# First norm's shift and scale weights of layer 0 in four units of two feature tiles, with four open sums in the first projection

## The chip, the cores and the metric

The kernel runs on one core of one Trainium2 chip. The metric is the device time of one execution in microseconds (us). The core's engines are TensorE (PE, matmuls; PEld its weight loads), VectorE (DVE), ScalarE (ACT) and GpSimd (POOL); SyncE (SP) issues nearly all DMAs, in program order on one queue.

## What is computed

A two-layer backbone over 256 latent and 256 context tokens with 1024 features. Layer 0 is a windowed attention and a bidirectional gated recurrence (HGRN2) side by side, layer 1 a retention; each layer ends with a SwiGLU feed-forward. Every sub-layer starts with an RMS norm whose result is modulated with a shift and a scale that come from a conditioning vector:

```python
for layer in range(DEPTH):
    m_lat = split((silu(c) @ mod_w[layer] + mod_b[layer]), 6)      # shift, scale, gate; shift, scale, gate
    m_ctx = split((silu(c_ctx) @ mod_w[layer] + mod_b[layer]), 6)
    h_lat = rms_norm(x, norm_g[layer, 0]) * (1.0 + m_lat[1]) + m_lat[0]
    h_ctx = rms_norm(ctx, norm_g[layer, 0]) * (1.0 + m_ctx[1]) + m_ctx[0]
    y_ctx, y_lat = mixer(h_ctx, h_lat, ...)                        # even or odd layer, h @ w_in first
    x = x + m_lat[2] * y_lat
    x = x + m_lat[5] * swiglu(rms_norm(x, norm_g[layer, 1]) * (1 + m_lat[4]) + m_lat[3], ...)
    # the same for ctx in layer 0
return x
```

## The kernel before

Activations lie with features on the 128 partitions: 8 feature tiles of 512 columns, 256 latent (`LAT`) and 256 context (`CTX`). All arithmetic is fp32. A dense product is made of three matmuls: each weight piece (8 blocks of 128x128, 512 KB, tile `raw`) is split into `whi` (ScalarE, L268) and `wlo` (VectorE, L269), each activation into `hh` or `u` (high) and `hl` or `u` (low), and L336, L337 and L338 multiply high by high, low by high and high by low. `ensure` makes the pieces `LOOK` = 2 ahead of the piece that is used; `raw` has three buffers, `whi` and `wlo` four. The order of the 230 pieces is the order in which `take` asks for them.

The start is written out by hand (`manual_schedule`), in the order in which each engine is to run it. SP loads constants (`con`), x (8 DMAs), the context (4 DMAs) and then `mw0`, the 8 MB of weights for layer 0's first shift and scale, as 32 tiles of 256 KB in four units: scale of feature tiles 0 to 3, scale of 4 to 7, shift of 0 to 3, shift of 4 to 7. ScalarE squares x and context, VectorE adds the squares, one matmul per stream with a matrix of ones sums them (L453), and Ln and Exp make 1/rms. `mod0a(nt)` multiplies the conditioning (`cT`, 32 columns) by a unit (L175, 8 matmuls), a copy takes the sum out of PSUM (L178), `mod0b(nt)` turns it into columns (L185, 4 matmuls of 2 columns) and adds the bias (L154, L158). `scaled` (L459) multiplies a feature tile by 1/rms and scale, `shifted` (L465, L466) adds the shift and splits it into `hh` and `hl`. Only then come the dense projections of the even layer:

```python
p1 = group('ein', [E_AK, E_AQ], K8, HS, sls=(LAT, CTX))
start('q', qk_post([(p1[0], 1, kt), (p1[1], 0, qt)]))
p2 = group('ein', [E_AQ + 1, E_AQ + 2, E_AQ + 3, E_AV], K8, HS, kouter=False)
```

The first has two columns of blocks in 128x256 halves, the second four columns of 128x512. The work that hangs on them runs in lanes (`qk_post`, `v_post`, the attention, the HGRN heads), generators that step once per tick; `work` makes a tick for every `TICK` = 1600 columns that the dense matmuls stream. The weights of the other shifts, scales and gates (`mwT`, 80 tasks of 512 KB) are reduced on VectorE at ticks too: `mod_tick` starts one task (two passes of L233 for the two streams) every `modt` ticks (`MODE` = 2.3 in the even layer; `MODT` later), and `mod_until` runs what is left of it at the end of a mixer. The token-major group (`tokgroup`, L409 to L411) follows the second projection. L567 and L578 are the small matmuls of `qk_post`, L483 is the residual update, L524 the silu of the conditioning `cb`.

Of the kernel before, what the change touches and what calls it, by code (L numbers as in the profile page):

```python
# [7 lines left out]
F32 = mybir.dt.float32  # L8
# [8 lines left out]
P = 128  # L17
# [18 lines left out]
MODT = [4.6, 5.5, 4, 4]  # L36
# [4 lines left out]
MODE = 2.3  # L41
# [27 lines left out]
def hybrid_kernel(ctx, tc, xT, wst, mw0, mwT, small, cbc, cst, imask, dmat, out, order):  # L69
# [47 lines left out]
    for i in range(32):
        if 16 <= i < 22:
            if i % 2 == 0:
                pair = rawp.tile([P, 2, NT], F32, tag="raw", name=nm("raw"))  # L120
            t = pair[:, i % 2, :]
        elif 22 <= i < 28:
            if i % 2 == 0:
                pair = mp.tile([P, D], F32, tag="mr", name=nm("mr"))
            t = pair[:, (i % 2) * NT:(i % 2 + 1) * NT]
        elif i < 16:
            t = u()[:]
        else:
# [42 lines left out]
    def mod0a(nt):  # L171
        ps = axb()
        for k in range(KD):
            g = k % 4
            T.matmul(ps[32 * g:32 * g + 32, :], cT[:, k, :], mws[nt * 8 + k], start=(k < 4), stop=(k >= 4),  # L175
                     skip_group_check=True)
        parts[nt] = u()
        A.activation(parts[nt][:], ps[:], AF.Copy)  # L178

    def mod0b(nt):  # L180
        ch, half = 1 - nt // 2, nt % 2
        part = parts[nt]
# [3 lines left out]
        mod_finish(0, ch, half * 4, half * 4 + 4, ps2[:].rearrange("p c s -> p s c"))  # L186
# [73 lines left out]

    def ensure(p):
        for q in range(len(pieces), min(p + LOOK, N_PIECE - 1) + 1):
            r = q
            load_raw(r)
            src = raws.pop(r)
# [153 lines left out]
    class Norm:  # L419
# [6 lines left out]
        def pre(self, k):  # L426
# [5 lines left out]
            A.activation(hi[:, LAT], x[k][:], AF.Copy, scale=g)  # L432
            V.scalar_tensor_tensor(lo[:, LAT], x[k][:], g, hi[:, LAT].bitcast(F32), ALU.mult, ALU.subtract)
# [98 lines left out]

# [786 lines left out]
```

## Time and profile before

| | us |
|---|---|
| median of three runs (lowest, highest) | 1146.19 (1146.14, 1147.27) |
| the profiled execution | 1146.45 |
| its span, first to last instruction | 1144.6 |
| PE busy in the span | 1116.4 (98%) |
| DVE busy | 767.4 (67%) |
| ACT busy | 554.0 (48%) |

Times in the rows are microseconds from the span's start. A matmul counts as busy for its modelled length, so a busy PE may still be waiting for a tick of another engine's work; the distance between starts is what a matmul costs. A fp32 matmul that is not split shows as two records.

### The profile page before, as it was taken

To read this page: it belongs to the slowest core of one execution; us is meant where nothing else is said; L and a number is where in the kernel's file an instruction comes from. 1 tells how busy PE (TensorE), PEld (TensorE's weight loads), DVE (VectorE), ACT (ScalarE), POOL (GpSimd) and SP (SyncE) were. 2 spreads that over 40 slices of the span, in tenths; PEclk is the share of its full clock that TensorE was granted. 3 is DMA by queue.
4 is the path that set the end of the run, shared out by engine and by line. 5 is a ranking of instruction groups with operands and counts; after the bars stand their busy time and mean duration, and the time that the engine had idled before them with its cause. 6 is when DMAs were issued, how large, how long until landed. Compare 5 with 4: busy or idle time off the path is not lost.

```text
span 1144.6 us, 18866 instructions
## 1 busy us (share of the span) xinstructions
PE 1116.4 (98%) x7514; PEld 996.9 (87%) x7514; DVE 767.4 (67%) x1399; ACT 554.0 (48%) x948; POOL 20.8 (2%) x46
## 2 busy tenths in 40 slices
PE   3999999999999999999999998999999999999998
PEld 1777877888998888988888898999999999999998
DVE  3877698899798557357883678374646577555553
ACT  5676676664753231123322476454445657544441
POOL 0012000000000000000000000000000000000000
PEclk9999999999999999999999999999999999999999
DMA  9987221326237446247983324343434265655553
GB/s 329 349 235 184 92 65 66 112 74 202 94 113 241 143 147 202 77 139 237 324 308 109 95 75 129 111 131 109 148 94 147 92 203 167 192 183 181 184 183 109
DMA packets 56121, 182.46 MB, mean 159 GB/s; under 512 B 6368, under 2 KB 9824, under 8 KB 55904
## 3 DMA queue, kind: packets, MB, share of 16 engines
q1 hardware_dynamic: 53648, 176.45, 47.6%
q0 software_dynamic: 2240, 4.72, 1.7%
q8 instruction: 59, 0.97, 0.4%
q14 instruction: 30, 0.25, 0.1%
q10 hardware_dynamic: 144, 0.08, 0.0%
HBM read 177.56 MB, written 1.05 MB: 156 GB/s over the span
## 4 chain that ended last, share of the span: by engine, by line
PE 84%; DVE 10%; ACT 3%; DMA 1%; issue 1%; DVEq 0%; ACTq 0%; SPq 0%
PE mm L338 23%; PE mm L337 23%; PE mm L336 23%; PE ax L337 2%; PE ax L336 2%; PE ax L338 2%; DVE wlo L269 2%; DMA raw<-in_wst_dram 1%; PE ax L175 1%; PE ax L656 1%; ACT whi L268 1%; PE ax L675 1%; DVE u L459 1%; PE mm L411 1%; PE mm L409 1%
## 5 line engine op out<-in xcount | busy, mean ns | idle before, releaser
L268 ACT ACTIVATE whi<-raw 128x1024 fp32r<-128x1024 f32 x230 | 243.3, 1059 | 403.0 <-PE mm L337 242.9
L269 DVE TENSOR_TENSOR wlo<-raw,whi 128x1024 fp32r<-128x1024 f32 x230 | 280.7, 1222 | 166.5 <-ACT whi L268 165.9
L336 PE MATMUL mm<-hh,whi 128*128 128x256 f32 (+1 forms) x1072 | 362.2, 339 | 1.2 <-ACT whi L268 0.9
L338 PE MATMUL mm<-hh,wlo 128*128 128x256 f32 (+1 forms) x1072 | 361.6, 338 | 0.6 <-DVE wlo L269 0.6
L337 PE MATMUL mm<-hl,whi 128*128 128x256 f32 (+1 forms) x1072 | 362.0, 338 | 0.1
L337 PE MATMUL mm<-u,whi 128*128 128x256 f32 (+2 forms) x768 | 236.9, 309 | 0.0
L338 PE MATMUL mm<-u,wlo 128*128 128x256 f32 (+2 forms) x768 | 236.7, 308 | 0.0
L336 PE MATMUL mm<-u,whi 128*128 128x256 f32 (+2 forms) x768 | 236.3, 308 | 0.3 <-DVE x L483 0.3
L338 PEld LDWEIGHTS mm<-hh,wlo 128*128 128x128 f32 x1072 | 204.4, 191 | 21.8 <-DVE wlo L269 0.8
L336 PEld LDWEIGHTS mm<-hh,whi 128*128 128x128 f32 x1072 | 204.2, 191 | 21.9 <-ACT whi L268 0.9
L337 PEld LDWEIGHTS mm<-hl,whi 128*128 128x128 f32 x1072 | 204.3, 191 | 20.2 <-DVE hl L466 0.3
L336 PEld LDWEIGHTS mm<-u,whi 128*128 128x128 f32 x768 | 146.4, 191 | 7.9 <-issue 0.4
L338 PEld LDWEIGHTS mm<-u,wlo 128*128 128x128 f32 x768 | 146.6, 191 | 7.2
L337 PEld LDWEIGHTS mm<-u,whi 128*128 128x128 f32 x768 | 146.6, 191 | 7.1
L233 DVE CUSTOM_DVE_ANT_0 mr<-mr,cb 128x1024 f32<-128x1024 f32 x72 | 87.1, 1222 | 13.2 <-DMA mr<-in_mwT_dram 12.6
L416 ACT ACTIVATE u<-u 128x512 fp32r<-128x512 f32 (+1 forms) x84 | 43.0, 526 | 36.7 <-DVE u L1007 17.3
L1007 DVE TENSOR_TENSOR u<-u,mm 128x512 f32<-128x512 f32 (+1 forms) x40 | 22.1, 553 | 44.7 <-PE mm L338 44.7
L233 DVE CUSTOM_DVE_ANT_0 u<-mr,cb 128x1024 bf16<-128x1024 f32 x40 | 48.4, 1219 | 2.8 <-DMA mr<-in_mwT_dram 1.5
L417 DVE TENSOR_TENSOR u<-u,u 128x512 fp32r<-128x512 f32 (+1 forms) x84 | 46.5, 565 | 5.0 <-ACT u L416 4.9
L336 PE MATMUL ax<-u,u 128*128 128x256 f32 x160 | 45.9, 287 | 3.1 <-ACT u L416 3.1
L483 DVE SCALAR_TENSOR_TENSOR x<-mm,modv,x 128x256 f32<-128x256 f32 x48 | 22.4, 480 | 36.1 <-PE mm L338 36.1
L337 PE MATMUL ax<-u,u 128*128 128x256 f32 x160 | 46.0, 287 | 0.0
(220 smaller groups left out, 1216.4 us busy)
## 6 DMA issues: line engine op xcount, KB each, us to landing
raw<-in_wst_dram SPq DMA_DIRECT2D x230, 512.0 KB, 3.8
mr<-in_mwT_dram SPq DMA_DIRECT2D x80, 512.0 KB, 4.5
u<-in_mw_dram SPq DMA_DIRECT2D x16, 256.0 KB, 5.2
u<-u POOLq DMA_DIRECT2D x20, 128.0 KB, 5.7
u<-in_dmat_dram POOLq DMA_DIRECT2D x8, 256.0 KB, 3.0
raw<-in_mw_dram SPq DMA_DIRECT2D x6, 256.0 KB, 5.2
mr<-in_mw_dram SPq DMA_DIRECT2D x6, 256.0 KB, 5.2
x<-in_xT_dram SPq DMA_DIRECT2D x8, 128.0 KB, 3.4
```

The costliest lines, as they stand in the source:

```text
L175: T.matmul(ps[32 * g:32 * g + 32, :], cT[:, k, :], mws[nt * 8 + k], start=(k < 4), stop=(k >= 4), skip_group_check=True)
L233: V.tensor_tensor_reduce(o, mr[:], cb[:, s, :], 1.0, 0.0, ALU.mult, ALU.add, mvec(l, s, ch, k))
L268: A.activation(hi[:], src[:], AF.Copy)
L269: V.tensor_tensor(lo[:], src[:], hi[:].bitcast(F32), ALU.subtract)
L336: T.matmul(o, w[0], a[0], start=first, stop=False, skip_group_check=shared)
L337: T.matmul(o, w[0], a[1], start=False, stop=False, skip_group_check=shared)
L338: anchor[0] = T.matmul(o, w[1], a[0], start=False, stop=last, skip_group_check=shared)
L409: T.matmul(ps[t][:], a[0], w[0], start=(k == 0), stop=False)
L416: A.activation(hi, src, AF.Copy)
L417: V.tensor_tensor(lo, src, hi.bitcast(F32), ALU.subtract)
L483: V.scalar_tensor_tensor(xs(m, s), ps[:, sl], mvec(l, s, ch, m), xs(m, s), ALU.mult, ALU.add)
L1007: V.tensor_tensor(g[:, 0:w], g[:, 0:w], ps[2 * i + 1][:, 0:w], ALU.mult)
```

## The change

`mw0` is stacked so that each of the four units holds the scale and the shift of two feature tiles. The loads stand in another order: unit 0, x in two DMAs, the context in four, then a weight piece and a unit in turn. The sums of squares go to PE (16 matmuls with the matrix of ones for two), ScalarE makes six of eight squares at 512 columns and VectorE two. Each unit is multiplied, and its two feature tiles are scaled and shifted, while the projection before it runs; this projection has four columns of 512 with four open sums over all k. It calls no `work`, so no tick passes in it. The second projection keeps two columns, `qk_post` is started three times for two, `lb_consts` moves ahead, and `MODE` and `MODT[0]` are 1.9 and 4.2 for 2.3 and 4.6.

```diff
-MODT = [4.6, 5.5, 4, 4]
+MODT = [4.2, 5.5, 4, 4]
-MODE = 2.3
+MODE = 1.9
...
+    def mw_load(p):
+        mws[p] = []
+        for i in range(KD):
+            if p < 3 or i >= 6:
+                t = u()[:]
+            else:
+                if i % 2 == 0:
+                    pair = mp.tile([P, D], F32, tag="mr", name=nm("mr"))
+                t = pair[:, i % 2 * NT:i % 2 * NT + NT]
+            nc.sync.dma_start(t, mw0[p, i])
+            mws[p].append(t)
+
+    mw_load(0)
+    for j in range(2):
+        nc.sync.dma_start(xl[j][:], xT[:, 0, 4 * j:4 * j + 4, :])
     for k in range(KD // 2):
-        nc.sync.dma_start(xc[k][:], xT[:, 2 * k:2 * k + 2, CTX])
+        nc.sync.dma_start(xc[k][:], xT[:, 1, 2 * k:2 * k + 2, :])
...
-        parts[nt] = u()
-        A.activation(parts[nt][:], ps[:], AF.Copy)
+        parts[p] = ps
+    def mod0b(p):
+        part = u()
+        A.activation(part[:], parts[p][:], AF.Copy)
...
+        for i, ch in enumerate((1, 0)):
+            mod_finish(0, ch, 2 * p, 2 * p + 2, ps2[:, 2 * i:2 * i + 2, :].rearrange("p c s -> p s c"))
...
+        load_raw(0)
+        for p in range(1, 3):
+            mw_load(p)
+            load_raw(p)
+        lb_consts()
+        mod0a(0)
+        mod0b(0)
+        stat = []
         for n in ns:
-            for k in range(KD):
-                n.add(k)
-            n.stats()
+            ps = axb()[:, 0:L]
+            for j in range(4):
+                q = u((P, 2, L))
+                src = xl[j // 2][:, 2 * (j % 2):2 * (j % 2) + 2, :] if n.s == 0 else xc[j][:]
+                if n.s and j % 2:
+                    V.tensor_tensor(q[:], src, src, ALU.mult)
+                else:
+                    A.activation(q[:], src, AF.Square)
+                for i in range(2):
+                    T.matmul(ps, ones, q[:, i, :], start=(j + i == 0), stop=(j + i == 4))
+            stat.append(ps)
+        for n, ps in zip(ns, stat):
+            n.r = u()[:, 0:L]
+            A.activation(n.r, ps, AF.Ln, bias=epst[:], scale=1.0 / D)
+            A.activation(n.r, n.r, AF.Exp, scale=-0.5)
+        p1 = [mmb() for _ in range(4)]
...
+        def dense(k, js):
+            for j in js:
+                w = take('ein', k, j)
+                o = p1[j][:]
+                T.matmul(o, w[0], HS[k][0], start=(k == 0), stop=False)
+                T.matmul(o, w[0], HS[k][1], start=False, stop=False)
+                anchor[0] = T.matmul(o, w[1], HS[k][0], start=False, stop=(k == KD - 1))
+
+        def feed(p):
+            for k in (2 * p, 2 * p + 1):
+                t = scaled(k)
+                if k == 2 * p:
+                    ensure(p)
+                shifted(k, t)
+
         mod0a(1)
-        mod0b(0)
-        scaled(0, range(4))
-        mod0a(2)
...
+        feed(0)
+        mw_load(3)
+        load_raw(3)
...
+        dense(0, J)
+        mod0b(1)
+        feed(1)
+        dense(1, J[:2])
+        mod0a(2)
+        dense(1, J[2:])
+        dense(2, J)
+        mod0b(2)
+        feed(2)
+        dense(3, J[:2])
+        mod0a(3)
+        dense(3, J[2:])
+        dense(4, J[:2])
+        mod0b(3)
+        feed(3)
+        dense(4, J[2:])
+        for k in range(5, KD):
+            dense(k, J)
...
-    p1 = group('ein', [E_AK, E_AQ], K8, HS, sls=(LAT, CTX))
     start('q', qk_post([(p1[0], 1, kt), (p1[1], 0, qt)]))
-    p2 = group('ein', [E_AQ + 1, E_AQ + 2, E_AQ + 3, E_AV], K8, HS, kouter=False)
-    start('q', qk_post([(p2[j], 0, qt) for j in range(3)]))
-    start('q', v_post(p2[3]))
+    start('q', qk_post([(p1[2], 0, qt), (p1[3], 0, qt)]))
+    p2 = group('ein', [E_AQ + 3, E_AV], K8, HS, kouter=False, banks=[axb(), mmb()])
+    start('q', qk_post([(p2[0], 0, qt)]))
+    start('q', v_post(p2[1]))
```

On ScalarE, ahead of the first weight piece: before, the squares, Ln and Exp of the latent stream stand ahead of those of the context (`u_199` to `u_219` and `u_228` to `u_248` are squares, `ax_222` and `ax_251` the sums), and four copies of `mod0a` follow. Before:

```order
L445 ACTIVATE u_219<-x_93 128x256
L289 ACT_TABLE_LOAD
L290 ACTIVATE u_224<-ax_222,eps 128x256
L456 ACT_TABLE_LOAD
L456 ACTIVATE u_224<-u_224 128x256
L445 ACTIVATE u_228<-u_94 128x256
...
L289 ACT_TABLE_LOAD
L290 ACTIVATE u_253<-ax_251,eps 128x256
L456 ACT_TABLE_LOAD
L456 ACTIVATE u_253<-u_253 128x256
L178 ACTIVATE u_280<-ax_271 128x512
```

Now (`ax_220` and `ax_237` are the two sums):

```order
L182 ACTIVATE u_210<-ax_201 128x512
L527 ACTIVATE u_221<-x_86 128x512
...
L527 ACTIVATE u_246<-u_90 128x512
L533 ACT_TABLE_LOAD
L533 ACTIVATE u_254<-ax_220,eps 128x256
L534 ACT_TABLE_LOAD
L534 ACTIVATE u_254<-u_254 128x256
L533 ACT_TABLE_LOAD
L533 ACTIVATE u_257<-ax_237,eps 128x256
L534 ACT_TABLE_LOAD
L534 ACTIVATE u_257<-u_257 128x256
L270 ACTIVATE whi_276<-raw_148 128x1024
```

The first copy has moved ahead of all squares, and all four table loads stand behind the squares, one stream's Ln and Exp directly behind the other's, with the first piece's split right after them.

On PE, the first dense matmuls. Before, all four units (L175) and their columns (L185) stand ahead of them:

```order
L175 MATMUL ax_330<-mw_167,cT 32x512
L175 MATMUL ax_330<-mw_169,cT 32x512
L185 MATMUL ax_341<-con,u_313 128x2 x4
L185 MATMUL ax_351<-con,u_339 128x2 x4
L336 MATMUL mm_431<-hh_183,whi_365 128x256
L336 MATMUL mm_432<-hh_183,whi_365 128x256
L337 MATMUL mm_431<-hl_184,whi_365 128x256
```

Now (L176 are a unit's matmuls, L185 its columns, L529 the sums of squares, `ax_220` of the latent and `ax_237` of the context stream, L552 to L554 the dense ones):

```order
L176 MATMUL ax_201<-u_109,cT 32x512
L185 MATMUL ax_212<-con,u_210 128x2 x4
L529 MATMUL ax_220<-u_221,con 128x256 x2
...
L529 MATMUL ax_237<-u_250,con 128x256 x2
L176 MATMUL ax_264<-u_150,cT 32x512
...
L552 MATMUL mm_260<-hh_132,whi_276 128x512
L553 MATMUL mm_260<-hl_133,whi_276 128x512
...
L554 MATMUL mm_263<-hh_132,wlo_277 128x512
L185 MATMUL ax_326<-con,u_324 128x2 x4
L552 MATMUL mm_260<-hh_134,whi_276 128x512
```

Only unit 0, the sums and unit 1 stand ahead of the first dense matmul now; the columns of unit 1 stand behind the dense matmuls of feature tile 0.

On DVE, the last adaLN passes of the even layer (`mod_until`; L233 before and L234 now, each followed by a short read of the sum, `modv 128x1`), between two splits of weight pieces. Before, from the split of piece 28 on:

```order
L269 TENSOR_TENSOR wlo_2861<-raw_2858,whi_2860 128x1024
...
L233 ISA u_2875,modv<-mr_2501,cb 128x1024
L233 ISA modv 128x1
L814 COPY u_2879<-ax_2878 128x128
L233 ISA mr_2501,modv<-mr_2501,cb 128x1024
...
L233 ISA u_2923,modv<-mr_2911,cb 128x1024
L233 ISA modv 128x1
L269 TENSOR_TENSOR wlo_2961<-raw_2958,whi_2960 128x1024
L233 ISA mr_2911,modv<-mr_2911,cb 128x1024
```

Now:

```order
L271 TENSOR_TENSOR wlo_2893<-raw_2890,whi_2892 128x1024
...
L234 ISA u_2821,modv<-mr_2666,cb 128x1024
L234 ISA modv 128x1
L865 SCALAR_TENSOR_TENSOR u_2796<-u_2796,ex_2572,ax_2795 128x128
L234 ISA mr_2666,modv<-mr_2666,cb 128x1024
...
L234 ISA u_2860,modv<-mr_2848,cb 128x1024
L234 ISA modv 128x1
L271 TENSOR_TENSOR wlo_2959<-raw_2956,whi_2958 128x1024
L234 ISA mr_2848,modv<-mr_2848,cb 128x1024
```

Between these two splits stand 7 passes before and 13 now; behind the second split 5 before and 3 now, so 12 and 16 in all.

## Rows read from the trace of the kernel before

**Rows 1.** The page's head and its busy time of PE over the whole span (us, share, instructions).

```profile
span 1144.6 us, 18866 instructions
PE 1116.4 (98%) x7514; PEld 996.9 (87%) x7514; DVE 767.4 (67%) x1399; ACT 554.0 (48%) x948; POOL 20.8 (2%) x46
```

**Rows 2.** PE's timeline of the first 40 us: start, length of the group, line, operation, count of records, and the idle time ahead with what ended it.

```profile
19.10 1.22 PE L453 MATMUL ax<-u,con 128*128 128x256 f32 x2 [6.54 <-DVE u L449]
20.25 5.73 PE L175 MATMUL ax<-u,cT 128*32 128x512 f32 x32
25.91 1.05 PE L185 MATMUL ax<-con,u 128*128 128x2 f32 x8
26.89 1.48 PE L175 MATMUL ax<-raw,cT 128*32 128x512 f32 x10
...
33.73 1.95 PE L185 MATMUL ax<-con,u 128*128 128x2 f32 x16
36.53 0.50 PE L336 MATMUL mm<-hh,whi 128*128 128x256 f32 x2 [0.85 <-ACT whi L268]
...
38.22 0.80 PE L338 MATMUL mm<-hh,wlo 128*128 128x256 f32 x2 [0.63 <-DVE wlo L269]
```

**Rows 3.** PE's waits from 45 us to the end, the longest: what for, us in total, times, longest.

```profile
PE ax L336 <- ACT u L416: 3.1, 1, 3.1
```

**Rows 4.** Four stretches of the start: length, PE's busy time (records), the granted clock of TensorE as a share of full speed, DMA share, GB/s.

```profile
20.00:35.00 15.00, 15.00 (x93) 1.00 1.05 409
35.00:38.00 3.00, 1.68 (x11) 1.00 1.04 398
38.00:42.00 4.00, 3.78 (x19) 0.57 1.03 423
42.00:50.00 8.00, 8.00 (x69) 1.00 0.89 344
```

**Rows 5.** DMA of 0 to 12 us and of 12 to 30 us (packets, megabytes, mean rate), SP's last issues of mw0 in its timeline, and the page's row of mw0's tiles (count, size, median us from issue to landing).

```profile
DMA packets 2706, 2.66 MB, mean 221 GB/s; under 512 B 235, under 2 KB 2539, under 8 KB 2706
...
DMA packets 4012, 7.31 MB, mean 406 GB/s; under 512 B 445, under 2 KB 445, under 8 KB 4012
...
25.61 2.27 SPq L130 DMA_DIRECT2D mw<-in_mw_dram  x4
...
u<-in_mw_dram SPq DMA_DIRECT2D x16, 256.0 KB, 5.2
```

**Rows 6.** ScalarE's timeline of the start.

```profile
3.71 1.28 ACT L167 ACT_TABLE_LOAD   x1 [3.71 <-DMA sml<-in_small_dram]
...
20.36 0.47 ACT L290 ACTIVATE u<-ax,eps 128x256 f32<-128x256 f32 x1 [1.81 <-PE ax L453]
20.85 1.28 ACT L456 ACT_TABLE_LOAD   x1
22.15 0.42 ACT L456 ACTIVATE u<-u 128x256 f32<-128x256 f32 x1
24.04 0.60 ACT L178 ACTIVATE u<-ax 128x512 f32<-128x512 f32 x1 [1.48 <-PE ax L175]
...
35.43 1.04 ACT L268 ACTIVATE whi<-raw 128x1024 fp32r<-128x1024 f32 x1
36.38 1.29 ACT L465 ACTIVATE hh<-u,modv 128x256 fp32r<-128x256 f32 x3
```

**Rows 7.** VectorE's timeline of the start.

```profile
27.40 1.67 DVE L459 SCALAR_TENSOR_TENSOR u<-x,gsv,u 128x256 f32<-128x256 f32 x4
...
36.95 1.21 DVE L269 TENSOR_TENSOR wlo<-raw,whi 128x1024 fp32r<-128x1024 f32 x1
...
40.41 4.83 DVE L466 SCALAR_TENSOR_TENSOR hl<-u,modv,hh 128x256 fp32r<-128x256 f32 x12
```

**Rows 8.** PE's timeline of the second projection: its first matmul, the small matmuls of `qk_post` in it, and the first matmul of the token-major group behind it.

```profile
50.82 0.40 PE L336 MATMUL mm<-hh,whi 128*128 128x512 f32 x1
...
56.06 1.02 PE L567 MATMUL ax<-u,u 128*128 128x512 f32 x2
...
57.15 1.02 PE L567 MATMUL ax<-u,u 128*128 128x512 f32 x2
...
63.05 0.59 PE L578 MATMUL ax<-u,u 128*128 128x256 f32 x2
...
63.71 0.59 PE L578 MATMUL ax<-u,u 128*128 128x256 f32 x2
...
75.30 0.39 PE L409 MATMUL mm<-whi,hh 128*128 128x512 f32 x1
```

**Rows 9.** Two stretches of the even layer: length, busy us (instructions) of PE, PEld, DVE, ACT and POOL, the granted clock, DMA share, GB/s.

```profile
50.00:140.00 90.00, 90.00 (x478) 71.85 (x477) 68.23 (x153) 59.22 (x112) 10.93 (x21) 1.00 0.64 182
140.00:280.00 140.00, 138.72 (x1152) 113.23 (x1151) 130.33 (x303) 91.04 (x206) 4.27 (x11) 1.00 0.30 95
```

**Rows 10.** DVE's groups of 256 to 274 us: count, busy us, mean ns, idle us ahead.

```profile
L233 DVE CUSTOM_DVE_ANT_0 u<-mr,cb 128x1024 bf16<-128x1024 f32 x6 | 7.2, 1219 | 0.1
L233 DVE CUSTOM_DVE_ANT_0 mr<-mr,cb 128x1024 f32<-128x1024 f32 x6 | 7.2, 1217 | 0.0
```

**Rows 11.** DVE's timeline behind them: the next split of a weight piece, and the first residual update of the even layer.

```profile
274.33 1.22 DVE L269 TENSOR_TENSOR wlo<-raw,whi 128x1024 fp32r<-128x1024 f32 x1
...
282.37 0.48 DVE L483 SCALAR_TENSOR_TENSOR x<-mm,modv,x 128x256 f32<-128x256 f32 x1
```

More of the change, by code (lines that the diff above doesn't have):

```diff
@@ L259, in load_raw @@
             raws[r] = t
+    look = [0]
     def ensure(p):
[L262 to L265, printed above, removed]
+        for q in range(len(pieces), min(p + look[0], N_PIECE - 1) + 1):
+            load_raw(q)
+            src = raws.pop(q)
             hi = wp.tile([P, PIECE, P], F32R, tag="whi", name=nm("whi"))
@@ L483, in upd, with lb_consts @@
         V.scalar_tensor_tensor(xs(m, s), ps[:, sl], mvec(l, s, ch, m), xs(m, s), ALU.mult, ALU.add)
+    omh = cp.tile([P, 4], F32, tag="omh", name="omh")
+    nomh = cp.tile([P, 4], F32, tag="nomh", name="nomh")
+    lbh = cp.tile([P, 4], F32, tag="lbh", name="lbh")
+    def lb_consts():
+        l0, l1 = sml[:, S_LB:S_LB + 4], sml[:, S_LB + 4:S_LB + 8]
+        mx, e0, e1 = sm(4), sm(4), sm(4)
+        V.tensor_tensor(mx, l0, l1, ALU.max)
+        V.tensor_tensor(e0, l0, mx, ALU.subtract)
+        V.tensor_tensor(e1, l1, mx, ALU.subtract)
+        A.preload_act_table_set("natural_log_exp_and_others")
+        A.activation(e0, e0, AF.Exp)
+        A.activation(e1, e1, AF.Exp)
+        V.tensor_tensor(e1, e0, e1, ALU.add)
+        V.reciprocal(e1, e1)
+        V.tensor_tensor(e0, e0, e1, ALU.mult)
+        V.tensor_scalar(omh[:], e0, -0.5, 0.5, ALU.mult, ALU.add)
+        V.tensor_scalar(nomh[:], e0, 0.5, -0.5, ALU.mult, ALU.add)
+        V.tensor_scalar(lbh[:], e0, 0.5, 0.5, ALU.mult, ALU.add)
     manual[0] = True
@@ new lines, in hybrid_kernel, with scaled, shifted @@
+        for n, ps in zip(ns, stat):
+            n.r = u()[:, 0:L]
+            A.activation(n.r, ps, AF.Ln, bias=epst[:], scale=1.0 / D)
+            A.activation(n.r, n.r, AF.Exp, scale=-0.5)
+        HS = [(a[:], b[:]) for a, b in h]
+        p1 = [mmb() for _ in range(4)]
+        def scaled(k):
+            t = u()
+            for n in ns:
+                n.scaled(k, t[:, n.sl])
+            return t
+        def shifted(k, t):
+            for n in ns:
+                n.shifted(k, t[:, n.sl])
@@ L1189, in hybrid_kernel @@
     for m in range(KD):
[L1190 removed]
+        nc.sync.dma_start(out[m * P:(m + 1) * P, :], x[m])
     assert len(order) == N_BLOCKS and mod_pos[0] == len(mod_tasks)
@@ L1266 @@
     cbc = np.stack([I['c'][0], I['c_ctx']])
-    m0 = mw[0][:, :2048].reshape(8, P, 4, 512)
-    mw0 = np.stack([m0[:, :, n] for n in (2, 3, 0, 1)])
+    m0 = mw[0][:, :2048].reshape(8, P, 2, 4, 256)
+    mw0 = np.stack([np.concatenate([m0[:, :, 1, p], m0[:, :, 0, p]], axis=2) for p in range(4)])
     mt = np.concatenate([mw[0].T[2048:], mw[1].T], axis=0).reshape(80, P, D)
```

82 lines of the change are left out of this document (13 added, 69 removed).

## The prediction

> **What bounds the kernel now.** The page comes first: TensorE (PE) is busy 98% of a span of 1144.6 us [rows 1], so a gain can only come from where PE lacks dense work. The list of what PE waits for after 45 us has 3.1 us as its longest entry [rows 3]; the start is what is left. In PE's timeline the first dense matmul starts at 36.53 and the first that has wlo at 38.22 [rows 2]; before them PE computes shift and scale from mw0. The last DMA of mw0 is issued by 27.9 and such a tile takes 5.2 us to land, so 33.1 [rows 5]; PE's last pieces of it (L185) start at 33.73 [rows 2]. So the start is bound by 8.4 MB of mw0 that must be in, whole, before any feature tile is normed. ScalarE's squares, Ln and Exp are over by 22.6 (22.15 and 0.42) [rows 6], so nothing but that transfer holds the norm up.
>
> PE starts the dense work with a low clock: granted 1.00 until 38, then 0.57 of full (mostly the 1.2 GHz level) for 4 us, after 3 us in which it was 56% busy, then 1.00 [rows 4]. That fall costs 4 x 0.43 = 1.7 us and is inside every later time.
>
> Behind the start, VectorE (DVE) is the second bound: busy 68.2 of 90 us between 50 and 140, and 130.3 of 140 between 140 and 280 [rows 9]. What PE gains early must pass through 140 us in which DVE has 9.7 us to spare.
>
> **The change, part by part: where the dense work starts.** 12 to 30 us, with mw0's rows of 2 KB, moved 406 GB/s; the stretch with x in rows of 1 KB moved 221 on the mean [rows 5]. Sml is in at 3.7 [rows 6], con beside it. At 406 a unit of 2.1 MB takes 5.2 us, so unit 0 is in at about 8.7, x (now rows of 4 KB) at 10.0 and 11.3, the context at 11.9 to 13.9, raw 0 at 15.2, unit 1 at 20.3, unit 2 at 27, unit 3 at 33.5. The nearest row for x by its place is 221 GB/s; with that for x and context alone they end 4.3 us later. I take 406, since rows are 2 KB or more.
>
> PE multiplies unit 0 as tiles land, done near 9.2; copy 0.60 [rows 6], L185 0.98 (25.91 to 26.89) [rows 2]: 10.8. Then come the sums of squares, which moved to PE: 16 fp32 matmuls of 128x256 where there were two and 14 DVE adds. One takes 1.15 us when PE comes from idling (19.10 to 20.25) [rows 2] and 0.43 at full speed (63.05 to 63.71 less one dense step of 0.228, below) [rows 8]. Bounds: 18.4 us and 6.9. Squares of 128x512 take about 0.6 by the copy's row, so ScalarE ends them near 13.7 and is no bound in the low case. From 19.10 on PE of before ran slowly for about 5 us: each fp32 matmul shows as two records, the ten records at 26.89 step by 0.10 (1.48 less 0.60 for the last, over nine), and the 32 of 20.25 in 5.1 us are then 3.9 us at 0.20 and the rest at 0.10, behind the 1.15 of L453 [rows 2]. Here unit 0 goes ahead, so I take 4 us at the slow price from 10.8 (3.5 matmuls) and 12.5 at 0.43: the latent sum at 16.8, the context's at 20.2.
>
> Ln and Exp of the two streams now stand behind one another on ScalarE, each with a table load: Ln 0.47, load 1.28, Exp 0.42 [rows 6]. From 16.8: Ln 17.3, load 18.5, Exp 19.0, load 20.2, Ln 20.7, load 22.0, Exp 22.4. These loads were hidden behind mw0; now three of them are on the path. Then whi 0 at 1.04 to 23.5, two hh at 0.43 (1.29 for three) [rows 6] to 24.3, beside them wlo 1.21 and two hl at 0.40 (4.83 for 12) [rows 7]: 25.5. So dense work starts at about 24.3 and is unhindered from 25.5, where it was 38.22.
>
> In these rows the load is followed 0.02 us after its end by its function (20.85 + 1.28, then 22.15) [rows 6]. The Trainium skill (ScalarE: Activation LUTs, What ACT_TABLE_LOAD costs) gives about 1.28 us for the load and 1.38 more for a drain with every switch. By that page three switches on the path would cost 4.1 us more and the sum below would end near 1145.5; no row here shows the drain, so I leave it out.
>
> **The first projections.** All four columns run over all k at 512 columns: 96 matmuls at 0.228 (50.82 to 75.30 is 24.48 us and holds 96 of them and four small matmuls, 2 x 0.86 and 2 x 0.43, 2.6 together) [rows 8]. From 25.5: 95 x 0.228 = 21.7, three L185 groups 2.9, two units of L175 at 16 records x 0.10 = 1.6 each: 3.2. Sum 53.3. Two columns remain, 48 x 0.228 = 10.9, and the 2.6 of small matmuls: 66.8. Before, this point is 75.30 [rows 8]. **Gain at the end of the projections: 8.5 us.**
>
> Cover in this stretch: a unit costs DVE three small operations, four scaled at 0.40 (27.40: 1.67 for four), a wlo and four hl, about 4.9 us [rows 7], and PE 2 x 2.73 + 0.98 + 1.6 = 8.1, so DVE keeps ahead by 1 us or so at each unit. SP's queue: raw 3 waits for wlo 0 and raw 4 for wlo 1, behind them stand the three constants, cb and the first mwT tiles; DVE has wlo 1 near 32, and raw 4 has 20 us from there to its use at 53.
>
> The clock: PE pauses between the sums and the dense start as it did between 35 and 38. A fall like that one costs 1.7 again, none costs 0; before holds one too, and my 66.8 holds none. I take 1.0. **7.5.**
>
> **What is given back.** The dense function makes no ticks, so ten ticks fewer have passed at the end of the projections, and the adaLN passes (L233, 1.22 each) and the lanes start later against PE. MODE 1.9 for 2.3 makes up for part: in the order, 16 passes are left behind piece 28's wlo where 12 stood. In the trace of before these 12 (six of either form) [rows 10] hold DVE until wlo at 274.33, eight us ahead of the first residual update at 282.37 [rows 11]. Four more are 4.9 us of DVE. Bounds: 0, if they fall into idle time, and 4.9. With 9.7 us idle in 140 [rows 9], most of it not at the end, I take 2.0. The attention lane, ten ticks later, now stands beside the HGRN lanes; its stall is between 0 and about 4 (of the 21.8 us that DVE idled before 140 [rows 9], PE's earlier pace takes 7.5 and leaves enough on the mean, not everywhere). I take 0.8. lb_consts, the earlier loads and the moved residual cost nothing: they lie in the wait for unit 0.
>
> **Sum.** 7.5 - 2.0 - 0.8 = 4.7 us. The profiled execution took 1146.45, the runs have a median of 1146.19: 1141.75 by the first, 1141.5 by the second; I give 1141.5.
>
> **The rivals.**
> B, nothing is given back. DVE has 31.4 us of idle time between 50 and 280 [rows 9], and 7.5 is a quarter of it. Against it: the last 140 us are 93% full. Time: 1146.2 - 7.5 = 1138.7; with sums at full speed throughout (1.9 less, then the table loads bound) 1136.8.
>
> C, the wait only moves. Either the sums run at half speed throughout: 18.4 us from 10.8 are 29.2, nine later than 20.2, and the dense work starts as late as before, about 1146. For it: PE idles or is paced by tiles before 10.8. Against it: the records of 20 to 25 us show it quick after some 4 us of work. Or DVE bounds the even layer outright, and 6 of the 7.5 are given back: 1144.7. For it: rows 9's 93%. So 1144 to 1146.5.
>
> D, slower: the granted clock falls again and again in the projection, where groups of 2-column matmuls (L185) and waits for hl interrupt the dense ones. One fall costs 1.7 [rows 4]; 4.7 + 2.3 over 1.7 is four more falls, from which the kernel would be slower; at the 1.2 GHz level from 25.5 to 53.3 it would end near 1169 (27.8 us more). Against it: from 42 us on the rows of before show 1.00 through small matmuls of the same sort [rows 4, 9]. The Trainium skill (TensorE: Matmul & The Clock Gate, HAM oscillation) describes such a loop, slow anew after each pause; by it only the pauses for hl matter, and I find none of over 1 us behind 25.5.
>
> **How the numbers follow.** The forecast (1139.5 to 1143.9) has 0.56, B 0.22, C 0.17, D 0.05. 0.2% is 2.3 us, about what a measurement of this kernel can tell from no change: faster is below 1143.9, the forecast and B, 0.78; C is no change, 0.17; slower 0.05. Leaving out the better half of B and the worst of C and D, the range is 1137.0 to 1145.0.
>
> **What would show it.** Dense from 24 to 26 us, with Exp of the context at 21 to 24 on ScalarE; the sums on PE ending at 19 to 22; first token group (L409's work) at 66 to 69 for 75.30; at most one stretch at half clock after 25; first residual update some 4 to 6 us ahead of 282.37. I am wrong if the sums take over 12 us, if PE waits for hl or wlo by more than 2 us in the projections, or if PE's list of waits from 140 to 280 grows by much over 3 us.

## The result, and the profile after

The changed kernel takes 1158.3 us (median of 4 runs, 1156.6 to 1160.4) where the kernel before, run beside it, takes 1146.7: a ratio of 1.010 with a 95% interval of 1.008 to 1.012. It is 11.5 us slower; 4.7 us faster was forecast. The profiled execution took 1159.8.

The page's head and PE's busy time, which answer to [rows 1]:

```profile
span 1158.0 us, 18795 instructions
PE 1127.8 (97%) x7494; PEld 1002.1 (87%) x7494; DVE 762.9 (66%) x1393; ACT 554.4 (48%) x941; POOL 20.9 (2%) x46
```

PE's timeline of the start, and the first matmul of the token group further on, for [rows 2, 8]:

```profile
13.01 7.15 PE L529 MATMUL ax<-u,con 128*128 128x256 f32 x32
20.10 2.84 PE L176 MATMUL ax<-u,cT 128*32 128x512 f32 x16
24.27 0.49 PE L552 MATMUL mm<-hh,whi 128*128 128x512 f32 x1 [1.33 <-ACT hh L467]
25.52 0.76 PE L553 MATMUL mm<-hl,whi 128*128 128x512 f32 x1 [0.76 <-DVE hl L468]
26.07 0.63 PE L554 MATMUL mm<-hh,wlo 128*128 128x512 f32 x1
...
29.04 0.39 PE L552 MATMUL mm<-hh,whi 128*128 128x512 f32 x1
...
69.27 0.40 PE L411 MATMUL mm<-whi,hh 128*128 128x512 f32 x1
```

The start came as forecast: dense work at 24.27 and, past the first hl, at 25.52. At 69.27 PE is 6.0 us ahead of before's 75.30. Everything was lost behind that point. PE's waits from 45 us to the end, where [rows 3] had 3.1 as the longest:

```profile
PE mm L339 <- DVE u L419: 3.5, 1, 3.5
PE ax L338 <- ACT u L418: 3.4, 1, 3.4
PE mm L338 <- DVE u L1056: 3.4, 1, 3.4
PE mm L338 <- ACT u L963: 1.8, 2, 1.0
PE mm L338 <- ACT u L951: 1.6, 1, 1.6
PE ax L816 <- ACT u L693: 1.6, 1, 1.6
PE mm L338 <- DVE u L442: 0.8, 2, 0.5
```

The second of these is the one that before has too, and the last stood there with 0.4. The rest is new; most of it names ScalarE, and what made ScalarE's results late is asked below. The starts of the same piece of work in the two traces (after less before, us; for the weight pieces the same matmul, counted from the end) put the losses in three places:

| point | before | after | difference |
|---|---|---|---|
| token group | 75.30 | 69.27 | -6.0 |
| output projection, first matmul on a lane's result (`mm<-u,whi`) | 257.18 | 258.66 | +1.5 |
| first residual update | 282.37 | 290.46 | +8.1 |
| first feed-forward, weight piece 80 | 559.3 | 567.3 | +8.0 |
| the same, weight piece 90 | 613.7 | 627.0 | +13.2 |
| weight piece 220 | 1112.2 | 1125.7 | +13.5 |

The rows of the second point, before and then after:

```profile
257.18 0.39 PE L336 MATMUL mm<-u,whi 128*128 128x512 f32 x1
```
```profile
258.66 0.39 PE L338 MATMUL mm<-u,whi 128*128 128x512 f32 x1
```

So 7.5 us go in the middle (token group to output projection), 6.6 in the tail of the mixer (output projection to residual update) and 5.2 in the first feed-forward; then nothing more. (Profiles differ by 13.4, the medians by 11.5.)

**The tail.** VectorE, the split of piece 29 and the residual update, which answer to [rows 11], with the last adaLN passes between them; PE at the wait; SP's queue ahead of it; ScalarE:

```profile
275.77 1.22 DVE L271 TENSOR_TENSOR wlo<-raw,whi 128x1024 fp32r<-128x1024 f32 x1
276.90 1.22 DVE L234 CUSTOM_DVE_ANT_0 mr<-mr,cb 128x1024 f32<-128x1024 f32 x1
278.05 0.08 DVE L234 DVE_READ_ACCUMULATOR2_ANT modv<- 128x1 f32 x1
278.05 1.22 DVE L234 CUSTOM_DVE_ANT_0 u<-mr,cb 128x1024 bf16<-128x1024 f32 x1
...
280.33 1.22 DVE L234 CUSTOM_DVE_ANT_0 mr<-mr,cb 128x1024 f32<-128x1024 f32 x1
281.48 0.08 DVE L234 DVE_READ_ACCUMULATOR2_ANT modv<- 128x1 f32 x1
281.48 0.69 DVE L419 TENSOR_TENSOR u<-u,u 128x512 fp32r<-128x512 f32 x1
...
290.46 0.48 DVE L485 SCALAR_TENSOR_TENSOR x<-mm,modv,x 128x256 f32<-128x256 f32 x1 [1.43 <-PE mm L340]
```
```profile
282.22 0.79 PE L339 MATMUL mm<-u,whi 128*128 128x512 f32 x1 [3.45 <-DVE u L419]
282.81 0.63 PE L340 MATMUL mm<-u,wlo 128*128 128x512 f32 x1
```
```profile
261.29 13.77 SPq L197 DMA_DIRECT2D mr<-in_mwT_dram  x6
277.05 0.33 SPq L259 DMA_DIRECT2D raw<-in_wst_dram  x1
```
```profile
281.53 1.06 ACT L270 ACTIVATE whi<-raw 128x1024 fp32r<-128x1024 f32 x1 [4.31 <-DMA raw<-in_wst_dram]
```

Between 258.6 and 281.5 VectorE runs 16 passes; the u that PE needs stands behind the last of them. While they run, six loads of `mr`, which wait for passes to free their buffers, hold SP for 13.8 us, and the weight pieces queue behind them; but VectorE has no gap of over 0.4 us in that stretch, so this u waits for the passes, not for the loads. In before all of the last 12 passes stand ahead of the split at 274.33 [rows 11]; of the 16 here three stand behind the split of the same piece, at 275.77. (The two listings of VectorE's order in the section on the change begin one piece apart: 246.9 us in before, 251.4 here.) After the wait PE works at a low clock.

**The first feed-forward.** VectorE's product in the feed-forward, behind two passes that end at 620.95, and PE's wait for it:

```profile
621.08 0.68 DVE L1056 TENSOR_TENSOR u<-u,mm 128x512 f32<-128x512 f32 x1
```
```profile
621.82 0.50 PE L338 MATMUL mm<-u,whi 128*128 128x512 f32 x1 [3.35 <-DVE u L1056]
```

Windows of PE's clock (columns as in [rows 9], the share of full speed third from the end):

```profile
25.00:30.00 5.00, 4.48 (x15) 3.64 (x15) 2.14 (x6) 2.34 (x4) 0.00 (x0) 0.66 1.05 409
30.00:50.00 20.00, 20.00 (x113) 14.12 (x114) 13.40 (x34) 9.42 (x17) 0.00 (x0) 1.00 0.90 345
280.00:290.00 10.00, 7.78 (x30) 6.68 (x31) 6.83 (x14) 1.78 (x3) 0.00 (x0) 0.66 0.81 270
620.00:630.00 10.00, 8.19 (x29) 6.62 (x30) 4.69 (x7) 1.69 (x2) 0.00 (x0) 0.83 0.18 61
```

**VectorE, where the loss begins.** The passes ahead of the token group, in before from 30 to 75.3 us (L233) and in after from 30 to 69.3 (L234); counts, duration, first and last start:

```profile
L233 DVE CUSTOM_DVE_ANT_0 u<-mr,cb x6: 1214/1218/1225, 47.6 to 73.2; 128x1024 bf16<-128x1024 f32 x6
L233 DVE CUSTOM_DVE_ANT_0 mr<-mr,cb x5: 1211/1217/1222, 49.9 to 74.4; 128x1024 f32<-128x1024 f32 x5
```
```profile
L234 DVE CUSTOM_DVE_ANT_0 u<-mr,cb x2: 1221/1222/1222, 58.6 to 61.0; 128x1024 bf16<-128x1024 f32 x2
L234 DVE CUSTOM_DVE_ANT_0 mr<-mr,cb x2: 1216/1221/1226, 59.9 to 66.1; 128x1024 f32<-128x1024 f32 x2
```

Windows from the first dense matmul to the token group, and from there to the first residual update, before and then after (length; PE, PEld, DVE, ACT busy):

```profile
36.50:75.30 38.80, 38.08 (x201) 32.73 (x201) 34.57 (x59) 28.55 (x43) 4.22 (x8) 0.96 0.84 274
75.30:282.40 207.10, 205.82 (x1527) 166.54 (x1526) 178.66 (x423) 135.45 (x297) 10.97 (x24) 1.00 0.40 119
```
```profile
24.30:69.27 44.97, 44.21 (x209) 33.17 (x209) 30.00 (x61) 27.88 (x42) 0.00 (x0) 0.96 0.76 278
69.27:290.46 221.19, 210.38 (x1537) 169.69 (x1536) 188.85 (x441) 138.55 (x302) 15.28 (x32) 0.98 0.42 126
```

In before VectorE idles 4.2 us in the first stretch, in after 15.0. PE was started 12 us earlier, and under that earlier work VectorE had too little that it could run: 7 passes of 1.22 (8.5 us) moved behind the token group, and VectorE has 188.9 us of work from there to the residual update instead of 178.7. Its idle time there didn't shrink: 28.4 and 32.3 us. So the stretch is 10.2 us longer by work and 3.9 by idle time, 221.2 for 207.1, and from a point 6.0 us earlier it ends 8.1 us later. That is bookkeeping and doesn't show yet that the work is the cause; the runs below do.

### The profile page after: what moved, and what is told of

Same layout as the page of the kernel before. It is cut to its first block, busy times and chain, and to the rows that moved or that the text cites. A ratio compares the mean times of both kernels' runs of the same rounds, so it can differ in the third digit from the quotient of the medians.

```text
span 1158.0 us, 18795 instructions
## 1 busy us (share of the span) xinstructions
PE 1127.8 (97%) x7494; PEld 1002.1 (87%) x7494; DVE 762.9 (66%) x1393; ACT 554.4 (48%) x941; POOL 20.9 (2%) x46
## 4 chain that ended last, share of the span: by engine, by line
PE 74%; DVE 13%; ACT 6%; DMA 4%; issue 2%; SPq 0%; DVEq 0%; ACTq 0%
PE mm L339 19%; PE mm L340 19%; PE mm L338 19%; DMA mr<-in_mwT_dram 4%; DVE wlo L271 3%; PE ax L339 2%; PE ax L338 2%; PE ax L340 2%; DVE mr L234 2%; ACT whi L270 1%; DVE hl L468 1%; DVE u L461 1%; PE ax L176 1%; PE ax L724 1%; PE mm L552 1%
## 5 line engine op out<-in xcount | busy, mean ns | idle before, releaser
L338 PE MATMUL mm<-hh,whi 128*128 128x512 f32 (+1 forms) x1016 | 344.3, 339 | 4.2 <-ACT u L963 1.8
L339 PE MATMUL mm<-hl,whi 128*128 128x512 f32 (+1 forms) x1016 | 342.9, 338 | 0.0
L340 PE MATMUL mm<-hh,wlo 128*128 128x512 f32 (+1 forms) x1016 | 342.3, 337 | 0.0
L338 PEld LDWEIGHTS mm<-hh,whi 128*128 128x128 f32 x1016 | 193.3, 190 | 24.9 <-ACT u L963 2.1
L340 PEld LDWEIGHTS mm<-hh,wlo 128*128 128x128 f32 x1016 | 193.3, 190 | 19.5
L339 PEld LDWEIGHTS mm<-hl,whi 128*128 128x128 f32 x1016 | 193.3, 190 | 18.5
L234 DVE CUSTOM_DVE_ANT_0 mr<-mr,cb 128x1024 f32<-128x1024 f32 x72 | 87.0, 1221 | 14.7 <-DMA mr<-in_mwT_dram 14.2
L234 DVE CUSTOM_DVE_ANT_0 u<-mr,cb 128x1024 bf16<-128x1024 f32 x40 | 48.4, 1219 | 1.4 <-DMA mr<-in_mwT_dram 1.2
```

The lines of the kernel that those rows point to most:

```text
L234: V.tensor_tensor_reduce(o, mr[:], cb[:, s, :], 1.0, 0.0, ALU.mult, ALU.add, mvec(l, s, ch, k))
L338: T.matmul(o, w[0], a[0], start=first, stop=False, skip_group_check=shared)
L339: T.matmul(o, w[0], a[1], start=False, stop=False, skip_group_check=shared)
L340: anchor[0] = T.matmul(o, w[1], a[0], start=False, stop=last, skip_group_check=shared)
```

## The experiments

The theories, as the expectations name them: L, the attention lane stands beside the HGRN lanes, ten ticks later; T, the adaLN passes packed ahead of the residual; D, VectorE's amount of work; F, passes that lag in the first feed-forward; N, the chain of each lane. Ratios are to the kernel before run beside each.

**L: the second `qk_post` in a lane of its own**, so that the attention steps at the weight blocks where before had them.

```diff
-    start('q', qk_post([(p1[2], 0, qt), (p1[3], 0, qt)]))
+    start('q2', qk_post([(p1[2], 0, qt), (p1[3], 0, qt)]))
```

> The changed kernel, but the second qk_post stands in a lane of its own, so that the attention steps again at the places of the dense work where they stood before the change (first step behind block 76 instead of 86, last behind 157 instead of 173); the adaLN tasks stay where the change put them. Theory L (the attention lane, pushed onto the HGRN lanes, costs the 7.4 us that PE loses between 70 and 250 us): 1158.3 - 7 = about 1151, and PE's waits for the softmax and the tanh between 150 and 216 us gone. Theory D (VectorE and ScalarE have no more to give, whatever the order; the gain of the start must be given back): within 2 us of 1158. Theory T (the late adaLN tasks do the damage): within 2 us of 1158.

Measured 1160.3, ratio 1.011 [1.010, 1.013]: no better. The waits came earlier (2.6 us for L629, 1.6 for L664), and behind the first the granted clock was 0.50 from 74 to 76 us; token group +0.9, output projection +2.6. As a remedy L falls: the gain is lost sooner, not saved. From token group to output projection this kernel takes 183.5 us, 181.9 in before and 189.4 in the changed one, so the run alone doesn't say that the lane's place has no part; the run on chunk 2 below leaves the lane late and takes 182.2.

**The ten ticks that the first projection no longer makes, given back at once to the counter of the passes.**

```diff
+    tickn[0] += 10
     start('q', qk_post([(p1[0], 1, kt), (p1[1], 0, qt)]))
```

> The changed kernel, but the task counter is set forward by the ten ticks that the first projection no longer makes, so the adaLN tasks of the even layer run early: six of the last 16 passes stand behind the split where the change has all 16, and none behind the next. The attention lane stays late. Theory T (the passes at the end of the even layer, with their loads in front of the next weight pieces on SP's queue, cost the 6.8 us between pieces 29 and 30): 1158.3 - 7 = about 1151, dense work past the first residual update without the wait of 3.5 us and without the fall of the clock behind it. Theory D: no change of over 2 us, since the same passes then burden 80 to 250 us. Theory L: no gain in the middle, the tail may or may not move.

Measured 1158.9, ratio 1.010 [1.008, 1.012]. The tail's wait is gone, but the first matmul on a lane's result starts at 271.02, 13.8 us after that of before. The passes now stand in a burst ahead of the lanes and waited for their loads: PE waited 4.2 us for `mr` and 3.6 for a copy, and its granted clock was 0.66, 0.85 and 0.64 in the three stretches of 10 us from 90 on. T alone doesn't explain the kernel. The loss moved from the tail to the middle, but by these waits and this clock, so the run doesn't show D's amount of work either.

**F: passes a little denser in the first feed-forward**, `MODT[1]` 5.3 for 5.5.

> The changed kernel with MODT[1] 5.3 for 5.5: the passes of layer 1's tasks then stand in the second half of the first feed-forward exactly where they stood before the change, two pieces earlier than with it (the counter of ticks enters the feed-forward 0.9 lower with the change). Theory F (these passes end too late for the feed-forward's last gate, which costs the 5.2 us between 560 and 630 us, a wait of 3.4 and a fall of the clock): 1158.3 - 5 = about 1153. Otherwise within 1 us of 1158.

Measured 1153.8, ratio 1.005 [1.003, 1.007]. The difference to before is +6.8 at the residual and +6.6 at pieces 80 and 90: the 5.2 us are gone. The change never touched this stretch; its counter enters 0.9 of a tick lower by the program's count, and in the traces the passes of the stretch's second half stand two pieces late, where this run has them as before. (Up to this stretch the program is that of the changed kernel, and its tail took 30.6 us for 31.8: two profiles of the same work differ by about 1 us.)

**T in the kernel before**: `MODT[0]` 6.0 for 4.6, which leaves 16 passes behind piece 28 there too.

> The kernel before with MODT[0] 6.0 for 4.6: nothing else of the change, but 16 of the late passes stand behind the split of piece 28, as with it, where before has 12. Theory T: the tail alone costs what it costs in the changed kernel, 4 to 7 us, so 1150 to 1153. Theory L or D: within 1 us of 1146.7, since the start, the lanes and the work in the middle are those of before.

Measured 1150.7, ratio 1.003 [1.002, 1.004]. Its first matmul on a lane's result and its first residual update:

```profile
256.04 0.39 PE L336 MATMUL mm<-u,whi 128*128 128x512 f32 x1
...
285.00 0.48 DVE L483 SCALAR_TENSOR_TENSOR x<-mm,modv,x 128x256 f32<-128x256 f32 x1 [0.89 <-PE mm L338]
```

The tail takes 29.0 us for before's 25.2: the burst costs 3.8 us by itself, more than half of the tail's 6.6.

**D at the tail: the 16 passes of chunk 4 over 8 columns**, in the changed kernel and in the one before. Such a pass leaves out 1016 of its 1024 columns.

```diff
+            if l == 0 and ch == 4:
+                V.tensor_tensor_reduce(o[:, 0:8], mr[:, 0:8], cb[:, s, 0:8], 1.0, 0.0, ALU.mult, ALU.add, mvec(l, s, ch, k))
+                continue
```

> The changed kernel with the 16 passes of chunk 4 (the second shift or scale of layer 0, the ones that stand at the even layer's end) over 8 columns instead of 1024, so these values are wrong; loads, queue order and everything else stay. About 16 us of VectorE's work are gone. Theory D (the end of the even layer is set by VectorE: the time of the token-major group's start, plus VectorE's work from there to the first residual update, plus some 30 us that it idles in every one of the kernels run so far; with the change that work is 188.9 us instead of 178.7): the first residual update comes at 272 to 277 for 290.5, where PE then bounds it, and the time is 1158.3 - 14 = 1142 to 1146. Theory T (only the tail suffers): 290.5 - 7, and 1151.

> The kernel before with the same 16 passes over 8 columns (those values are wrong). Theory D: VectorE alone would allow the first residual update at 75.3 + 162.7 + 30 = 268 for 282.4, PE then bounds it before that: 276 to 282, and 1141 to 1146. So by D the changed kernel with short passes is ahead of this one by about the 6 us of its start at the first residual update. Theory T: no gain of over 1 us, since before shows next to no wait in the tail.

Measured 1153.8, ratio 1.005 [1.004, 1.007], and 1145.3, 0.999 [0.998, 1.000]. In the changed kernel the first residual update comes at

```profile
282.73 0.48 DVE L488 SCALAR_TENSOR_TENSOR x<-mm,modv,x 128x256 f32<-128x256 f32 x1 [1.32 <-PE mm L343]
```

for 290.46. The tail takes 23.1 us here and 23.6 in before with the same edit, so its loss is gone, but neither that of the middle (output projection +2.4) nor that of the feed-forward (4.6 between pieces 80 and 90). D, as I had put it (work taken away anywhere in the even layer comes back as time), was too strong: work counts where it stands.

**Chunk 4 on PE**, in both kernels (`PES = [3, 4]`, `MODT[0]` 2.6, and in the changed one `MODT[1]` 5.3).

> The changed kernel with chunk 4's tasks on PE, as chunk 3's are (PES = [3, 4]; 16 passes of VectorE become 4 x 24 small records on PE and 4 x 3 small operations), at MODT[0] 2.6 so that they come before the tail, and with MODT[1] 5.3 of the feed-forward experiment. Theory D: VectorE loses 18 us of work, PE gains 4 x 2 = 8 us, of which part lies in its waits: first residual update at 274 to 282 for 290.5, time 1158.3 - 5 - 8 to 14 = 1139 to 1146. Theory T: the tail's 6.8 and the feed-forward's 5.2 come back, and PE's own work of up to 8 is added: 1147 to 1154.

> The kernel before with the same chunk on PE and MODT[0] 2.6. Theory D: before was bound by PE and VectorE about equally, so VectorE's relief is worth little and PE's 8 us of small matmuls cost: 1144 to 1153. The changed kernel with this edit is then ahead by the start's 6 us or some of it.

Measured 1147.7, ratio 1.0005 [0.9996, 1.0015], and 1152.0, 1.004 [1.003, 1.006]. With VectorE relieved, the changed kernel is 4.3 us faster than the old one with the same chunk on PE, and 6.8 ahead at the first residual update (279.99 and 286.81); the two differ in `MODE` and `MODT[1]` as well as in the start. PE pays for the relief: from token group to output projection either kernel takes some 6 us more than before (188.0 and 188.2 for 181.9), about what the new matmuls keep PE busy there (13.0 us for 6.5).

**D against N in the middle: chunk 2's passes over 8 columns**, the edit above with `ch == 2`.

> The changed kernel with the 16 adaLN passes of chunk 2 (the even layer's gate, made at ticks between 58 and about 150 us) over 8 columns for 1024, which leaves out most of that sum; every instruction keeps its place. VectorE loses some 16 x 1.1 = 17.6 us of work in the middle and none in the tail. In the changed kernel the middle (token group at 69.3 to the fourth piece of the output projection at 250) lost 7.4 us against before, and the tail 6.8. Theory D (VectorE's work bounds the middle): the first pieces of the output projection, which start 1.4 us later than before's now, start 4 to 7 us earlier than before's, and since the passes of the tail keep their places the tail's wait grows or shrinks little: 1147 to 1153. Theory N (the middle is bound by the chain of each lane, with the results of the first projection no earlier than before): output projection at +0 to +2, time 1156 to 1159.

Measured 1151.7, ratio 1.005 [1.003, 1.006]. First matmul on a lane's result:

```profile
249.89 0.39 PE L341 MATMUL mm<-u,whi 128*128 128x512 f32 x1
```

7.3 us ahead of before's 257.18 for 1.5 behind it; the start's whole gain arrives. Token group to output projection takes 182.2 us, before's 181.9, with lanes and weight blocks where the change put them. N falls, and the middle's loss hangs on VectorE's passes, though the waits named ScalarE. The edit takes away some 17 us, twice what had moved, and the kernel before wasn't run with it; what the moved passes alone are worth is shown below. The tail (3.5 us for the same u, L422 here) and the feed-forward then lose 5.4 and 6.9.

**Two tasks (four passes) put under the first projection**, with `MODT[1]` 5.3.

```diff
+        A.activation(cb[:], cb[:], AF.Silu)
         mod0b(3)
...
             dense(k, J)
-        A.activation(cb[:], cb[:], AF.Silu)
+            if k > 5:
+                mod_one()
```

> The changed kernel with MODT[1] 5.3 (1153.8 us by itself) and, beside it, two adaLN tasks (four passes) made by hand behind feature tiles 6 and 7 of the first projection, with the silu of the conditioning moved ahead of the last unit's copy: VectorE's idle time of 44 to 58 us takes them, and two tasks fewer stand behind piece 28. All else is kept. Before made 11 passes ahead of its token group and the changed kernel 4; this one should make some 8. Theory D: four passes are 4.9 us of VectorE, so the first residual update comes 3 to 5 us earlier and the time is 1149 to 1151. Theory N: the middle stays as late, only the tail gains by 4 passes of its 16: 1151 to 1154. The passes could also hold back the splits of pieces 4 and 5, which have 9 to 12 us of lead: no loss expected there.

Measured 1149.0, ratio 1.0015 [1.0006, 1.0025]. Output projection 3.0 us ahead of before, though the token group is at -4.4 only: the silu held up the last unit's copy, and PE waited 2.0 us for it.

**`MODT[1]` 5.1 with chunk 4 on PE, and with the early tasks as well.**

> The changed kernel with chunk 4 on TensorE and MODT[0] 2.6 (1147.7 us by itself, equal to before), with MODT[1] at 5.1 for 5.3. In that kernel the second half of the first feed-forward still loses 2.4 us between pieces 80 and 90. Theory F (passes lag behind there): the 2.4 us go, 1145 to 1146. If the loss has another cause: 1147.5 or more.

> The last one with the two early tasks of the third run of this set as well. D: chunk 2 is all that VectorE still has in the middle, and two of its eight tasks leave it: output projection 1 to 3 us earlier than without, 1142.5 to 1145. N: no change against the kernel without the early tasks.

Measured 1147.4 [0.9995, 1.0015] and 1152.5 [1.003, 1.006]. The first shows no gain. The loss between pieces 80 and 90 that the expectation names isn't there in the run it starts from: by the matmuls of the table above that kernel stands at +0.6 at both, this one at 0.0 at both. What both lose, 3.0 us, lies between the first residual update and piece 80; 1.4 of it is a wait of PE for the feed-forward's first silu (L1055). The second misses: the same silu costs 4.7 us by the token group, and nothing comes back behind it (189.3 us to the output projection for 188.0); why not isn't shown.

**The early tasks without that wait**: the load of `cb` ahead of piece 3's, its silu behind the split of piece 2, where ScalarE idled; two tasks, three, and three with `MODT[0]` 3.8.

```diff
         mw_load(3)
+        nc.sync.dma_start(cb[:], ...)
         load_raw(3)
...
                     ensure(p)
+                    if p == 2:
+                        A.activation(cb[:], cb[:], AF.Silu)
```

> As the run with two early adaLN tasks (1149.0 us), but the load of the conditioning is issued ahead of piece 3 and its silu stands behind the split of piece 2, where ScalarE idles for 3.4 us. Theory D (VectorE's passes, put back where it idled, win the middle back): no wait for the copy of the last unit, token group 6 to 7.5 us before that of before as in the changed kernel, output projection 5 to 6.5 us before it for 3.0, 1145 to 1147. If the better middle was only the later token group: output projection at -3, 1149.

> The same with three early tasks (behind feature tiles 5, 6 and 7) and MODT[1] 5.4. Six passes are 7.3 us of VectorE, of which 5 or so are idle time and the rest comes out of the lead of the splits (9 to 12 us); the tail keeps 10 passes behind piece 28 where the changed kernel has 16. D: output projection 5.5 to 7 us before that of before, first residual update 3 to 5 us before, no loss in the feed-forward, 1142 to 1145. Otherwise 1147 to 1149.

> The last one with MODT[0] 3.8 for 4.2: of chunk 4's passes 8 stand behind piece 28 and none of the burst of 9 ahead of piece 29. T (the burst in the tail costs by itself): 1 to 3 us faster than with 4.2. D in its narrow sense (only the amount of work counts): the same within 1 us.

Two tasks: 1145.85, ratio 0.9989 [0.9980, 0.9999], the only kernel here that computes all and is ahead of before, by 1.3 us and hardly more than can be told. Its two windows (columns as above), its first matmul on a lane's result and its first residual update:

```profile
24.80:68.20 43.40, 42.64 (x208) 31.99 (x209) 33.87 (x67) 28.20 (x42) 1.04 (x2) 1.00 0.83 303
68.20:278.10 209.90, 206.45 (x1525) 165.99 (x1524) 183.74 (x435) 136.40 (x299) 15.17 (x32) 1.00 0.40 121
...
251.45 0.39 PE L338 MATMUL mm<-u,whi 128*128 128x512 f32 x1
...
278.08 0.48 DVE L485 SCALAR_TENSOR_TENSOR x<-mm,modv,x 128x256 f32<-128x256 f32 x1
```

VectorE idles 9.5 us for 15.0 under the first projections, and the output projection comes 7.2 us earlier (251.45 for 258.66) from 4.9 us of passes: 1.1 by the token group, 6.2 in the middle. Not all of it lasts: 4.3 us ahead of before at the residual update, 1.3 at piece 80 of the feed-forward. 1.4 of these 3.0 us are PE's wait at 350.29 for the feed-forward's first silu (L1058), which neither before nor the changed kernel has. Three tasks: 1148.1, ratio 1.0008 [0.9998, 1.0019]; spread: 1149.8, 1.002 [1.001, 1.003]. Both missed. With three tasks PE's list begins with

```profile
PE mm L338 <- ACT u L954: 3.6, 1, 3.6
```

at 99 us, a copy of the token group's result (L951 in after, 1.6 us there). ScalarE ahead of it, and PE's clock behind it:

```profile
95.44 1.06 ACT L270 ACTIVATE whi<-raw 128x1024 fp32r<-128x1024 f32 x1 [1.00 <-PE mm L413]
...
98.40 0.59 ACT L954 ACTIVATE u<-mm 128x512 f32<-128x512 f32 x1
```
```profile
100.00:110.00 10.00, 10.00 (x36) 7.89 (x35) 3.99 (x9) 4.47 (x11) 2.03 (x4) 0.70 0.64 167
```

With three tasks a split of a weight piece stands ahead of the copy on ScalarE and waits for PE; with two that split runs behind the copies, at 98.11. The wait is 2.0 us longer and the clock costs some 3 (10 x 0.30, an estimate), of the 8.1 us that this kernel's middle is longer than with two tasks (191.3 for 183.2); the rest stays open. So it isn't the amount of VectorE's work alone; spreading the tail's passes gained nothing either.

## Why the prediction was wrong

**The start came out right, in part by luck.** Sums end at 20.10 (20.2 forecast), but they start at 13.01 for 10.8 and take 7.1 us for 9.4: no matmul of them ran at the slow price (granted clock 1.00 from 13 to 20), and two errors of over 2 us cancel. From there the sum holds: the dense work starts at 24.27 and 25.52 (24.3 and 25.5). The table loads, three of the four on the path, cost what [rows 6] said:

```profile
15.42 1.28 ACT L533 ACT_TABLE_LOAD   x1
16.75 0.48 ACT L533 ACTIVATE u<-ax,eps 128x256 f32<-128x256 f32 x1
```

A function follows its load 0.05 us after the end. The extra drain that the Trainium skill gives (ScalarE: Activation LUTs, What ACT_TABLE_LOAD costs) isn't seen in these rows, and leaving it out was right.

**The clock** fell once in the projections: seven matmuls from 26.07 to 29.04 at 0.43 for 0.23 are 1.4 us, 1.0 was taken. Token group: 66.8 + 1.4 = 68.2 with the fall as measured, 69.27 in the trace; most of the rest is that units 2 and 3 cost PE 2.1 us each for 1.6. The start's gain was 6.0, not 7.5.

**"What is given back" failed**, 2.8 us for 19.5. Three terms:

- *Lanes and middle*, 0.8 taken, 7.5 measured. I looked only at passes behind piece 28 and found four more. Ahead of the token group there were seven fewer, and they had to be made in a stretch that VectorE already filled to 86% (178.7 of 207.1). The idle time there didn't take them up: it was 28.4 us before and 32.3 after. Rival B leaned on it, and so did my 0.8. Two early tasks, 4.9 us of passes put back, shortened the middle by 6.2. The text named the ticks that no longer pass, and its own cover sum (8.1 us of PE against 4.9 of VectorE for each unit) had VectorE idle under the new first projection; it never asked which passes would be missing there.
- *Tail*, 2.0 taken with 4.9 as the bound, 6.6 measured. The passes by themselves are 3.8 (16 behind piece 28 in before), there with a wait of 2.7 and the granted clock at 1.00 from 280 to 290. Here the wait is 3.45 and the clock is low to about 288 (0.63 records for 0.39), which the sum held nothing for; why the wait is longer isn't shown.
- *First feed-forward*, nothing taken, 5.2 measured: the counter of ticks came in lower, and the passes stood two pieces late in a stretch where they had no spare time.

**The rivals.** C, second form (VectorE bounds the even layer and 6 of 7.5 are given back), had the right mechanism, and its price was a third of the real one: it let VectorE's work stay the same in amount. D had a falling clock in the projection: the window from 30 to 50 us shows 1.00 there. The clock did fall elsewhere, behind waits of 3.4 us on other engines. No rival had slower by way of VectorE, and that was the case that came. Of the signs of being wrong the last came: from 140 to 280 us PE idles 7.0 us for 1.3 in before.

## What to carry to other kernels

When an engine is let start earlier, write down for every other engine what it has to do in the new stretch: idle time there is work that comes due later, and if that engine is the second bound the gain can be lost again. Count moved periodic work (passes at ticks) at every point of the program against before, not only at its end, and follow the counter's phase into the stages behind. The idle share of an engine that feeds waiting lanes wasn't free capacity here; try the move with the work put where the idle time is, and look at what then stands in front of what on the other engines: a third task put there cost more than it gave.

## What was not expected of the hardware

Two waits of PE of about 3.4 us cost more than themselves: the granted clock was 0.66 from 280 to 290, around the end of the one at 282, and 0.83 from 620 to 630, around that of the one at 621. From 282.81 to about 288 the matmuls show 0.63 us for 0.39 at full speed. Shorter waits did not all do the same: behind 2.6 us in the run with the lane of its own the clock was 0.50 (74 to 76 us), behind 2.7 us in the kernel before with the late burst it was 1.00 (280 to 290). And 16 passes cut to 8 columns, some 17 us less work for VectorE, made the kernel before only about 2 us faster (1145.3 for 1147.6 by the medians): there PE had hardly waited for them.
